# Third mixer of a four-layer block: moving the last channel tile, the value projection and the convolution's layer norm between the attention heads

## The chip, the cores and the metric

One core of a Trainium2 chip runs the whole program in one launch. The metric is the device time of one execution in microseconds (us). The engines are TensorE (PE, matrix products and transposes; PEld is its weight load), VectorE (DVE), ScalarE (ACT), GpSimd (POOL) and SyncE (SP, which here only issues transfers). PE writes into PSUM, which the kernel divides into eight banks of 128 x 512 floats.

## What is computed

A residual stream of 512 positions by 1024 channels passes four layers. The third layer's mixer, the one that the change touches, computes differential attention in 4 heads beside a convolution over 512 channels. Cut to what matters:

```python
def even_mixer_2(t, ...):
    proj = t @ w_in                                   # q, k, v, and a, g for the convolution
    y_a = diff_attention(proj[..., :3 * DIFF_WIDTH], ...)
    y_b = conformer_conv(proj[..., 3 * DIFF_WIDTH:], dw_w, dw_b, ln_g, ln_b)
    return jnp.concatenate([y_a, y_b], axis=-1) @ w_out

def diff_attention(...):     # 4 heads, two score maps each
    sc = jnp.einsum('bqhcd,bkhcd->bhcqk', qb, k) * scale
    p = jax.nn.softmax(jnp.where(chunk_causal_mask(i, s), sc, -jnp.inf), axis=-1)
    w = p[:, :, 0] - lam * p[:, :, 1]
    o = jnp.einsum('bhqk,bkhe->bqhe', w, v)
    ...
    o = rmsnorm(o, subln) * (1.0 - lam_init)

def conformer_conv(g, dw_w, dw_b, ln_g, ln_b):
    u = g[..., :CONV_CHANNELS] * jax.nn.sigmoid(g[..., CONV_CHANNELS:])
    y = lax.conv_general_dilated(u, dw_w, ...) + dw_b  # 31 taps, each channel by itself
    return jax.nn.silu(layernorm(y, ln_g, ln_b))
```

## The kernel before

Every projection is made in three passes over rounded parts of its operands (`mm3`, L143 to L149: high times high, high times low, low times high), so 512 columns against 1024 rows of input cost 8 x 3 matmuls. `projT` (L155) gives channels on the partitions, `projS` (L168) positions on the partitions. `wload` (L122) loads a piece of weights over SP into `wr`, ACT casts it to the high part (L133) and DVE subtracts to get the low part (L116).

The Python text is not the order in which the engines work. A framework places every instruction on its engine's queue: it goes by rank, which is the place in the program's text (moved ahead by `prio(n)`, behind by a negative one), and takes the first in rank that is ready on its own clock. Each queue then runs in the order so fixed, and semaphores guard the data. `hold` (L269) adds an edge of order without a semaphore. So work that stands later in the text fills the gaps of work that stands earlier. Buffers come from rings: 14 large tiles (`A4`), 13 of 512 columns (`U`), and PSUM banks in four rings, P (2), Z (3), W (2) and O (1).

`even2` (L722 to L899) is the third mixer. Its parts:

- `projT("e2t", ...)` with `conv` (L768) makes the convolution's input in four channel tiles of 128; the sigmoid is L777, the product `up` L778. Tiles 0 to 2 are convolved on DVE, 31 taps each (`taps`, L787 to L790), at low rank. Tile 3 goes to PE: `shifted` (L743) writes `up` to DRAM (L747), reads it back as four shifted copies `cu` (L752), and `conv_pe` (L758) makes 32 matmuls into bank O, `pc` (L764), which DVE adds to `ycv` (L766).
- `scores(h)` (L815) makes head h's two score maps in four blocks of 128 positions: products into two Z banks (L822), maximum and exponential (`softmax_rows`, L416 to L420), scaling and difference (L827 to L831), transposes into a W bank (`pw`) and a copy into `wt` (`evac_wt`, L361).
- `projS("e2v", ...)` (L885) is the value projection, through the two P banks. `av_(h)` (L839) multiplies `wt` with `v` into bank P (even heads) or O (odd heads), `po` (L368); ACT squares it (L378) and copies it (L379), DVE sums (L380).
- `stats` (L842) transposes `ycv` through W banks (L847), ACT copies to `yS` and squares (L849, L851). `norm` (L858) is the layer norm's root and the scaling (L861). `silu` (L863) transposes back through W banks, applies SiLU (L870) and splits into the two parts `mh`, `ml`.
- `heads` (L873) divides by the heads' norm (`over_rms`, L391), transposes through W banks, scales and splits (L881, L882). Then `outp` multiplies the mix with the output weights; `y` needs all eight banks, and its first channel tiles are the convolution's (order 4, 5, 6, 7, 0, 1, 2, 3). Four of its weights are cast into large tiles, `wb`.

The order of the text at the end of `even2` is scores(0), value projection, scores(1), channel tile 3, scores(2), av_(0), av_(1), the convolution on PE, scores(3), av_(2), stats, av_(3), norm, silu, heads.

Of the kernel before, what the change touches and what calls it, by code (L numbers as in the profile page):

```python
# [50 lines left out]
class Net:  # L51
# [670 lines left out]
    def even2(self):  # L722
        nc = self.nc
# [31 lines left out]
            nc.sync.dma_start(dwd, self.A["dwd"])  # L755
            cp[t] = us, dwd.rearrange("p a (m g c) -> p (a m) g c", g=4, c=32)

        def conv_pe(t):  # L758

            us, dwd = cp[t]  # L760
            pc = self.bank("O", "pc")
            for m in range(8):
                for g in range(4):
                    nc.tensor.matmul(pc[32 * g : 32 * g + 32], lhsT=dwd[:, m, g], rhs=us[g][:, 4 * m : 4 * m + 512],  # L764
                                     start=m == 0, stop=m == 7)
            V.tensor_scalar(ycv[:, t], pc, self.v("db", t), None, ALU.add)  # L766

        def conv(i, ps):  # L768
# [46 lines left out]
        def scores(h):  # L815
            wt = self.A4(name="wt")
            for tb in range(NB):
                N = (tb + 1) * P
                es = []
                rr = self.st(2, "rr")  # L820
                pss = [self.bank("Z", "sc") for _ in range(2)]
                self.pair([lambda r=slice(64 * c, 64 * c + 64), ps=ps: nc.tensor.matmul(  # L822
                    ps[:, :N], lhsT=qk[0][r, h, tb * P : N], rhs=qk[1][r, h, :N], start=True, stop=True) for c, ps in enumerate(pss)])
                for c, ps in enumerate(pss):
                    e, sm = self.softmax_rows(ps, N)
                    self.freed = self.freed or self.last_e
                    V.reciprocal(rr[:, c : c + 1], sm)  # L827
                    es.append(e)
                V.tensor_scalar(rr[:, 1:2], rr[:, 1:2], nlam, None, ALU.mult)
                nc.scalar.activation(es[0][:, :N], es[0][:, :N], AF.Copy, scale=rr[:, 0:1])  # L830
                V.scalar_tensor_tensor(es[0][:, :N], es[1][:, :N], rr[:, 1:2], es[0][:, :N], ALU.mult, ALU.add)  # L831
                self.evac_wt(wt, es[0], tb)
            wts.append(wt)
# [5 lines left out]
        def av_(h):  # L839
            self.head(h, wts[h], v, on, ss, "PO"[h % 2])  # L840

        def stats():  # L842

            for tb in range(NB):
                pt = self.bank("W", "pt")
                for k in range(4):
                    self.tr(pt[:, k * P : k * P + P], ycv[:, k, tb * P : tb * P + P])  # L847
                c = slice(tb, tb + 1)
                nc.scalar.activation(yS[:, tb], pt, AF.Copy, accum_out=sm[:, c])  # L849
                V.tensor_scalar(nm[:, c], sm[:, c], -1.0 / 512, None, ALU.mult)  # L850
                nc.scalar.activation(self.junk(512), yS[:, tb], AF.Square, bias=nm[:, c], accum_out=sq[:, c])  # L851
# [3 lines left out]
        def mix_half(i):  # L855
            self.mh[i], self.ml[i] = self.A4(F32R, "mh"), self.A4(F32R, "ml")

        def norm():  # L858
            r = self.rstd_v(sq, 4, 512, LN_EPS)
            for tb in range(NB):  # L860
                V.tensor_scalar(yS[:, tb], yS[:, tb], nm[:, tb : tb + 1], r[:, tb : tb + 1], ALU.add, ALU.mult)  # L861

        def silu():  # L863
            mix_half(1)
            for k in range(4):
                pt = self.bank("W", "pt")
                for tb in range(NB):
                    self.tr(pt[:, tb * P : tb * P + P], yS[:, tb, k * P : k * P + P])
                m = self.U(name="m")
                nc.scalar.activation(m, pt, AF.Silu, bias=self.v("lnb", k), scale=self.v("lng", k))  # L870
                self.split(*self.mix(4 + k), m)

        def heads():  # L873
            mix_half(0)
            self.over_rms(on, ss)
            for h in range(4):
                pt = self.bank("W", "pt")
                for tb in range(NB):
                    self.tr(pt[:, tb * P : tb * P + P], on[:, tb, h * P : h * P + P])
                mh, ml = self.mix(h)  # L880
                nc.scalar.activation(mh, pt, AF.Copy, scale=sub)  # L881
                V.scalar_tensor_tensor(ml, pt, sub, mh.bitcast(F32), ALU.mult, ALU.subtract)  # L882

        scores(0)
        self.projS("e2v", 512, lambda tb, ps: nc.scalar.copy(v[:, tb], ps))  # L885
        scores(1)
        self.projT("e2t", range(6, 8), conv)
        scores(2)
        av_(0)
        av_(1)  # L890
        conv_pe(3)
        scores(3)
        av_(2)
        stats()
        av_(3)
        norm()
        silu()
        heads()
        self.order = [4, 5, 6, 7, 0, 1, 2, 3]  # L899

# [546 lines left out]
```

## Time and profile before

| what | us |
|---|---|
| median of 3 runs (1713.58 to 1717.89) | 1717.76 |
| the profiled execution | 1711.21 |
| its span | 1709.4 |
| PE busy | 1656.5 |
| DVE busy | 950.2 |
| ACT busy | 677.7 |
| mean granted clock of PE (1 is full) | 0.987 |

The span is the time between the profile's first and last instruction; the execution has 1.8 us around it. Matmuls are pipelined and their ends are modelled, so a busy PE is not one at its peak. The third mixer's heads lie between about 607 and 710 us of the span.

### The profile page before, as it was taken

The page shows a single profiled execution, that of the slowest core. Times are in us where ns is not written, and L with a number is a line of the kernel's source. Part 1 is how long each engine was busy: PE and PEld are TensorE (multiplying, and loading weights), DVE is VectorE, ACT ScalarE, POOL GpSimd, SP SyncE. Part 2 cuts the span into 40 slices and gives each one's busy share as a digit, 9 for nine tenths or more (in the row PEclk, how much of TensorE's full clock was granted, in tenths as well). Part 3 has the DMA queues.
Part 4 walks back from the last instruction along what each step waited for, and adds up shares of the span by engine and source line. Part 5 has one row for each costly group of instructions (what it writes and reads, how often), then busy time and mean ns, then how long its engine had stood idle before and what let it go on. Part 6 is the DMA issues. An engine that isn't in the chain of part 4 may idle for free.

```text
span 1709.4 us, 20684 instructions
## 1 busy us (share of the span) xinstructions
PE 1656.5 (97%) x8072; PEld 1323.6 (77%) x8072; DVE 950.2 (56%) x1801; ACT 677.7 (40%) x1192; POOL 2.0 (0%) x8
## 2 busy tenths in 40 slices
PE   8999999999999999799999999999889999999998
PEld 8657788987789775588888878886447988888886
DVE  7564456765667994663222288468695622224332
ACT  6453334214545254643222254334556522223231
POOL 0000000000000000000000000000000000000000
PEclk9999999999999998899999999999999999999999
DMA  5212252202153220252222246432005332222341
GB/s 203 85 38 74 91 181 105 75 25 99 62 205 116 74 87 33 84 187 99 99 99 97 91 151 200 165 123 81 31 31 197 111 100 99 99 95 90 99 160 50
DMA packets 53169, 179.07 MB, mean 105 GB/s; under 512 B 5696, under 2 KB 8256, under 8 KB 52944
## 3 DMA queue, kind: packets, MB, share of 16 engines
q1 hardware_dynamic: 43824, 146.20, 25.6%
q10 hardware_dynamic: 9216, 31.48, 4.9%
q8 instruction: 63, 1.03, 0.2%
q14 instruction: 34, 0.28, 0.1%
q0 software_dynamic: 32, 0.07, 0.0%
HBM read 159.63 MB, written 18.10 MB: 104 GB/s over the span
## 4 chain that ended last, share of the span: by engine, by line
PE 85%; DVE 7%; ACT 4%; DMA 2%; issue 1%; ACTq 0%; DVEq 0%; SPq 0%
PE pp L145 17%; PE pp L148 17%; PE pp L149 17%; PE y L145 7%; PE y L149 7%; PE y L148 7%; PE pt L203 2%; PE po L368 2%; PE pl L625 1%; PE pw L203 1%; PE sc L822 1%; PE po L481 1%; DMA wr<-in_e2out 1%; PE pc L764 0%; DMA nw<-in_nw 0%
## 5 line engine op out<-in xcount | busy, mean ns | idle before, releaser
L116 DVE TENSOR_TENSOR wl<-wr,wh 128x1024 fp32r<-128x1024 f32 (+2 forms) x224 | 271.3, 1213 | 343.8 <-ACT wh L133 338.5
L133 ACT CAST wh<-wr 128x1024 fp32r<-128x1024 f32 (+2 forms) x224 | 233.4, 1043 | 523.4 <-PE pp L148 399.2
L148 PE MATMUL pp<-xl,wh 128*128 128x512 f32 (+1 forms) x1184 | 428.5, 362 | 0.0
L145 PE MATMUL pp<-xh,wh 128*128 128x512 f32 (+1 forms) x1184 | 426.0, 361 | 1.2 <-ACT xh L235 1.2
L149 PE MATMUL pp<-xh,wl 128*128 128x512 f32 (+1 forms) x1184 | 425.8, 360 | 0.0
L145 PEld LDWEIGHTS pp<-xh,wh 128*128 128x128 f32 x1184 | 223.8, 190 | 35.6 <-ACT xh L235 2.5
L148 PEld LDWEIGHTS pp<-xl,wh 128*128 128x128 f32 x1184 | 224.7, 190 | 33.8 <-issue 1.9
L149 PEld LDWEIGHTS pp<-xh,wl 128*128 128x128 f32 x1184 | 224.4, 190 | 33.4 <-issue 2.1
L145 PE MATMUL pp<-wh,xh 128*128 128x512 f32 (+1 forms) x320 | 126.4, 395 | 1.4 <-ACT sg L777 1.4
L148 PE MATMUL pp<-wl,xh 128*128 128x512 f32 (+1 forms) x320 | 126.5, 395 | 0.0
L149 PE MATMUL pp<-wh,xl 128*128 128x512 f32 (+1 forms) x320 | 125.4, 392 | 0.0
L145 PE MATMUL y<-wh,ah 128*128 128x512 f32 x288 | 112.7, 391 | 0.2
L148 PE MATMUL y<-wl,ah 128*128 128x512 f32 x288 | 112.3, 390 | 0.0
L149 PE MATMUL y<-wh,al 128*128 128x512 f32 x288 | 112.2, 389 | 0.0
L1238 DVE TENSOR_TENSOR act<-g,pp 128x512 f32<-128x512 f32 x44 | 30.2, 686 | 132.8 <-PE pp L149 131.4
L145 PEld LDWEIGHTS pp<-wh,xh 128*128 128x128 f32 x320 | 60.2, 188 | 13.4 <-ACT sg L777 1.8
L148 PEld LDWEIGHTS pp<-wl,xh 128*128 128x128 f32 x320 | 60.3, 188 | 11.7 <-issue 1.1
L149 PEld LDWEIGHTS pp<-wh,xl 128*128 128x128 f32 x320 | 60.2, 188 | 11.5 <-issue 0.6
L145 PEld LDWEIGHTS y<-wh,ah 128*128 128x128 f32 x288 | 54.1, 188 | 12.4 <-ACT bbz L998 1.1
L322 DVE TENSOR_TENSOR yn<-y,nw 128x512 f32<-128x512 f32 x48 | 31.8, 686 | 56.9 <-ACT yn L320 52.7
L790 DVE SCALAR_TENSOR_TENSOR ycv<-up,vec,ycv 128x512 f32<-128x512 f32 x90 | 63.2, 739 | 0.4
L149 PEld LDWEIGHTS y<-wh,al 128*128 128x128 f32 x288 | 54.1, 188 | 11.1
(381 smaller groups left out, 2335.0 us busy)
## 6 DMA issues: line engine op xcount, KB each, us to landing
wr<-in_f0gu SPq DMA_DIRECT2D x44, 512.0 KB, 3.3
wr<-in_f1gu SPq DMA_DIRECT2D x44, 512.0 KB, 3.3
wr<-in_f0d SPq DMA_DIRECT2D x22, 512.0 KB, 3.6
wr<-in_f1d SPq DMA_DIRECT2D x22, 512.0 KB, 3.4
xd<-x ACTq DMA_DIRECT2D x20, 512.0 KB, 2.7
x<-xd ACTq DMA_DIRECT2D x20, 512.0 KB, 6.1
wr<-in_o1t SPq DMA_DIRECT2D x16, 512.0 KB, 3.6
nw<-in_nw ACTq DMA_DIRECT2D x12, 512.0 KB, 7.8
```

What stands on the lines that cost most here:

```text
L116: return self.nc.vector.tensor_tensor(l, src, h.bitcast(F32), ALU.subtract)
L133: c = nc.scalar.copy(h, raw)
L145: r = mm(out, lhsT=a[0], rhs=b[0], start=first, stop=False)
L148: mm(out, lhsT=a[0], rhs=b[1], start=False, stop=False)
L149: return mm(out, lhsT=a[1], rhs=b[0], start=False, stop=last)
L203: self.nc.tensor.transpose(out, in_, self.ident)
L322: nc.vector.tensor_tensor(yn[j], yb[b][j], postw[j], ALU.mult)
L368: self.nc.tensor.matmul(po[:, tb * P : tb * P + P], lhsT=wt[:, sb, tb * P : tb * P + P], rhs=v[:, sb, c], start=sb == 0, stop=sb == tb)
L481: nc.tensor.matmul(po[r, sb * P :], lhsT=sv[:, sb, h * 64 : h * 64 + 64], rhs=wt[:, sb, sb * P :], start=sb == 0, stop=sb == 3)
L625: nc.tensor.matmul(pl[:, c4 * 64 : c4 * 64 + 64].rearrange("p (n x) -> p n x", x=H), lhsT=k[:, c4 * P : c4 * P + P], rhs=rh, start=True, s ...
L790: V.scalar_tensor_tensor(y, up[:, j : j + 512], self.v("dw", 4 * j + t), y, ALU.mult, ALU.add)
L1238: nc.vector.tensor_tensor(act[k // 4][:, k % 4], g, ps, ALU.mult)
```

## The change

The calls at the end of `even2` are reordered: channel tile 3 comes behind scores(0), the convolution on PE and then the value projection behind scores(1), layer norm (`stats`, `norm`) behind scores(2), `silu` behind scores(3) and ahead of the value products 1 to 3. The convolution gets an edge of order: its first matmul of each of the four column groups is placed behind the last exponential of the head whose scores were written last in the text, head 1.

```diff
-        def conv_pe(t):
+        def conv_pe(t, after):
...
-                    nc.tensor.matmul(pc[32 * g : 32 * g + 32], lhsT=dwd[:, m, g], rhs=us[g][:, 4 * m : 4 * m + 512],
-                                     start=m == 0, stop=m == 7)
+                    r = nc.tensor.matmul(pc[32 * g : 32 * g + 32], lhsT=dwd[:, m, g], rhs=us[g][:, 4 * m : 4 * m + 512],
+                                         start=m == 0, stop=m == 7)
+                    if m == 0:
+                        self.hold(r, after)
...
         scores(0)
+        self.projT("e2t", range(6, 8), conv)
+        scores(1)
+        conv_pe(3, self.last_e)
         self.projS("e2v", 512, lambda tb, ps: nc.scalar.copy(v[:, tb], ps))
-        scores(1)
-        self.projT("e2t", range(6, 8), conv)
         scores(2)
+        stats()
+        norm()
         av_(0)
+        scores(3)
+        silu()
         av_(1)
-        conv_pe(3)
-        scores(3)
         av_(2)
-        stats()
         av_(3)
-        norm()
-        silu()
         heads()
```

## Rows read from the trace of the kernel before

**Rows 1.** The page, engines: busy us, share of the span, instructions.
```profile
PE 1656.5 (97%) x8072; PEld 1323.6 (77%) x8072; DVE 950.2 (56%) x1801; ACT 677.7 (40%) x1192; POOL 2.0 (0%) x8
```
**Rows 2.** Stretches: start:end, length, busy by engine (instructions), PE clock, DMA share, GB/s.
```profile
607.70:652.50 44.80, 44.70 (x203) 31.86 (x202) 37.14 (x100) 25.70 (x59) 0.00 (x0) 1.00 0.24 77
652.50:673.20 20.70, 17.46 (x87) 11.29 (x90) 10.07 (x38) 11.30 (x29) 0.00 (x0) 0.74 0.18 67
673.20:681.60 8.40, 8.40 (x66) 2.11 (x65) 1.08 (x5) 1.69 (x6) 0.00 (x0) 0.83 0.01 2
681.60:692.60 11.00, 8.64 (x48) 5.29 (x45) 8.06 (x26) 7.42 (x20) 0.00 (x0) 1.00 0.00 1
692.60:710.10 17.50, 10.32 (x51) 8.36 (x50) 10.65 (x39) 12.92 (x28) 0.00 (x0) 0.71 0.00 0
710.10:757.50 47.40, 46.59 (x217) 37.56 (x217) 29.07 (x42) 25.38 (x43) 0.00 (x0) 1.00 0.53 189
```
**Rows 3.** PE in order of time: start, us, line, tile out<-in, count [idle before].
```profile
652.47 0.49 PE L822 MATMUL sc<-kT,qT 64*128 64x128 f32 x4
652.89 4.73 PE L368 MATMUL po<-v,wt 128*128 128x128 f32 x40
...
673.13 8.48 PE L764 MATMUL pc<-cu,dwd 128*32 128x512 f32 x64
...
681.80 0.70 PE L822 MATMUL sc<-kT,qT 64*128 64x256 f32 x4
...
692.40 0.60 PE L203 MATMUL pt<-cst,ycv 128*128 128x128 f32 x4
...
702.07 1.96 PE L203 MATMUL pt<-cst,yS 128*128 128x128 f32 x8 [6.29 <-DVE yS L861]
```
**Rows 4.** Stretches, the clock: as in rows 2.
```profile
662.00:673.00 11.00, 9.28 (x27) 4.90 (x26) 5.58 (x19) 6.05 (x14) 0.00 (x0) 0.52 0.19 70
...
678.00:680.00 2.00, 2.00 (x24) 0.60 (x20) 0.00 (x0) 0.00 (x0) 0.00 (x0) 1.00 0.04 8
```
**Rows 5.** ACT in order of time, 624 to 712 us: columns as in rows 3.
```profile
624.66 0.59 ACT L885 COPY v<-pp 128x512 f32<-128x512 f32 x1 [1.45 <-PE pp L149]
...
653.19 1.28 ACT L420 ACT_TABLE_LOAD   x1
654.49 0.37 ACT L420 ACTIVATE e<-sc,nm 128x128 f32<-128x128 f32 x1
...
692.60 0.59 ACT L361 COPY wt<-pw 128x512 f32<-128x512 f32 x1 [1.08 <-PE pw L203]
...
698.48 0.59 ACT L378 ACTIVATE sq<-po 128x512 f32<-128x512 f32 x1
...
703.86 1.45 ACT L870 ACTIVATE m<-pt,vec 128x512 f32<-128x512 f32 x2 [3.01 <-PE pt L203]
705.20 1.13 ACT L119 CAST mh<-m 128x512 fp32r<-128x512 f32 x2
...
710.11 1.46 ACT L881 ACTIVATE mh<-pt,lqt 128x512 fp32r<-128x512 f32 x2 [1.40 <-PE pt L203]
711.46 2.93 ACT L133 CAST wb<-wr 128x1024 fp32r<-128x1024 f32 x3
```
**Rows 6.** DVE in order of time, first mixer, then third: columns as in rows 3.
```profile
222.71 0.17 DVE L194 TENSOR_SCALAR h<-hs 128x16 f32<-128x16 f32 x1
...
225.09 2.50 DVE L391 TENSOR_TENSOR oret<-oret,r 128x512 f32<-128x512 f32 x4
...
643.48 0.68 DVE L790 SCALAR_TENSOR_TENSOR ycv<-up,vec,ycv 128x512 f32<-128x512 f32 x1
...
653.39 0.68 DVE L778 TENSOR_TENSOR up<-sg,pp 128x512 f32<-128x512 f32 x1
```
**Rows 7.** SP's issue of `cu`, and GB/s in 40 slices of 654 to 672 us.
```profile
656.23 2.54 SPq L752 DMA_DIRECT2D cu<-cvd  x4
GB/s 0 0 338 281 0 0 0 0 0 0 101 96 82 96 101 96 96 101 96 96 101 101 96 96 101 106 101 101 101 106 96 96 101 96 86 14 0 0 0 0
```

## Prediction, made before the changed kernel was run

> **What bounds the kernel now.** The first page says that TensorE (PE) is busy for 97% of the span [rows 1]; a matmul-bound kernel can only gain where PE stands still or runs at its lower clock. So the second view is the table by stretches of the third mixer's end [rows 2], read for PE busy against length, and for the clock. From 607.7 to 652.5 us PE is full (44.70 of 44.80 us): heads 0 and 1 lie over the value projection and the last channel tile. From 710.1 us, in the output projection, it is full again (46.59 of 47.40). Between them lie 57.6 us with all the slack: head 2 (20.7 us, mean clock 0.74), the convolution as a block (8.4), the rest of head 3 (11.0) and the tail (17.5, PE busy 10.32, clock 0.71). I then read the orders of PE, ScalarE (ACT) and VectorE (DVE) in these stretches [rows 3, 5, 6].
>
> Four things stand out. One: the convolution block runs from 673.13 for 8.48 us, and head 3's next scores come only at 681.80 [rows 3]; meanwhile ACT is busy 1.69 us and DVE 1.08 of 8.4 [rows 2]. Two: the `ycv` transposes of the layer norm start at 692.40, after head 3's last scores, and the `yS` transposes at 702.07 after a 6.29 us wait [rows 3]. Three: ACT serves the last value product (`sq<-po`) only at 698.48, after the norm's passes [rows 5]. Four: the first head transpose is read at 710.11 and the weights `wb` are cast right behind it, at 711.46 [rows 5]. I take 710.11 as the milestone: what follows it hangs on it, through `wb` and through the W banks that the head transposes leave to `y`.
>
> **The change, part by part.** Nothing is removed or added except one ordering edge; three things move. PE's work is the same, so the sum is one of waits.
>
> (1) *Channel tile under head 0, value projection under head 1.* Each is filler of PE behind scores of higher rank; PE was full and stays so, with one exception. The projection's two P banks are held until `up` is written: 652.47 to 653.39 + 0.68 = 654.07 us in the trace [rows 3, 6], 1.6 us, covered there because PE had `po` in the O bank. After the change the value projection needs those P banks, and ACT must also switch its table for the sigmoid. Bounds 0 (head 1's scores fill it) and 2.9 (1.6 plus a table load of 1.28 [rows 5]); I take 1.5. The cover of DVE's taps (last row at 643.48 [rows 6]) is not lost: the taps still lie under heads 0 and 1, and the layer norm, which needs them, comes only behind head 2. On SP and in ACT's casts the tile's two pieces of weights swap places with the projection's four, the same number of each: nothing, as both are prefetched under the key projection.
>
> (2) *Convolution after head 1's last exponential.* It goes in front of the remaining value projection, on a PE that is at full clock: 64 instructions at the 24 per 2 us of 678 to 680 [rows 4] are 5.3 us; in place they took 8.48 [rows 3], at a mean clock of 0.83 [rows 2]. Between these bounds I take 6.0, nearer to the warm row. Its four `cu` loads need time: issued from 656.23, they move data until slice 35 of 40 of the DMA row, 670.2, which is 16 us after `up` [rows 7]. The channel tile takes the place of the first half of the value projection, which ended at 624.66 [rows 5]; a table load, the sigmoid and `up` on top make 627.5, so the loads land near 643.5. Head 1 can start at 625 too and, at 2.0 + 11.0 us for a head at full clock (part 3), has its last exponential near 638.5. On SP the block's six transfers also move past the prefetch of output weights, which can hold them while it waits for a buffer. PE is in order, so if the block is queued behind that exponential, the value projection behind it waits: bounds 0 and 5; I take 1.5, since there is other work that can be put in front. Head 2 then starts at 652.5 + 1.5 + 6.0 + 1.5 = 661.5 (before 652.47).
>
> (3) *Heads 2 and 3.* They took 652.5 to 692.6, 40.1 us [rows 2]. Off: the block, 8.4. Back on: head 3's first softmax that ran beneath the block, for which ACT was busy 1.69 us there [rows 2]: 2.0. Off: a part of the 4.73 us of `po` that stood in front of head 2's second score block [rows 3], since `v` is now fresh and the product no longer gets there first: bounds 0 and 3, I take 2. The clock: it was 0.52 from 662 to 673 [rows 4], after thin PE work, and came back only inside the block; head 3 then ran at 1.00 [rows 2]. Without the block nothing dense stands between the heads, so head 3 probably runs at the lower clock. Head 2 from 657.6 to 673.2 needed 15.6 us at it, head 3 from 681.6 to 692.6 needed 11.0 at full clock: bounds 0 and 4.6, I take 2.5. The layer norm's first half (16 transposes; ACT 4 copies and 4 squares, 5.3 us, from the copy's end at 692.60 + 0.59 to 698.48 [rows 5]) now stands in ACT's queue between heads 2 and 3, with head 3's exponentials behind it. ACT is idle for 9.4 of head 2's 20.7 us [rows 2], so bounds 0 and 5.3; I take 2. Sum: 40.1 - 8.4 + 2.0 - 2.0 + 2.5 + 2.0 = 36.2, so head 3's last copy comes at 697.7 (before 692.60, [rows 5]).
>
> (4) *The tail, from that copy to the first head transpose read, 17.5 us before.* The norm's 5.3 us of ACT and its DVE chain leave it. What is late next is `silu`, which the change ranks ahead of the value products 1 to 3. ACT: copy 0.5, table load 1.28, four `m` and four `mh` (1.45 + 1.13 for two [rows 5], 5.2) = 7.0; then square and copy of product 2 and the square of product 3 (0.59 each [rows 5], 1.6 with their overlap); the sum on DVE, one pass of 0.68; the 16-wide root alone 2.4 (222.71 to 225.09 in the first mixer) and the four products 2.5 [rows 6]; four transposes 0.60 [rows 3]. Together 14.8. Lower bound 8.6, if ACT takes the last product before `silu`: copy 0.6, half a product 1.2 (4.73 us were two, [rows 3]), square 0.6, then the same 6.2. Upper 19 (second rival). The milestone: 697.7 + 14.8 = 712.5, +2.4 us.
>
> (5) *Output projection.* `silu`'s tiles come first in its order and are ready well before the milestone, but that is no gain: `y` of the last row block needs the W banks and `wb` comes behind the heads, so PE can do the first tile's matmuls alone, which it does now too, and then pauses. The block before shows what a restart costs: a mean clock of 0.83 over 8.4 us [rows 2] is 1.4 us lost. Bounds 0 and 1.4; I take 0.6.
>
> In all +3.0 us. The profiled execution took 1711.2 (span 1709.4 and 1.8 around it), so 1714.2; the median of the runs, 1717.8, lies 6.6 above it, and I carry the difference over: **1720.8**.
>
> **A rule against the change.** Rows first: the switch from sigmoid to exponential at 653.19 costs one load of 1.28 us, and the exponential starts at its end, at 654.49 [rows 5]. The Trainium skill ("ScalarE: Activation LUTs", Rules for kernel authors) says to do all functions of one table set before switching, and under "What ACT_TABLE_LOAD costs" it gives about 2.66 us for a switch, a drain of 1.38 included. By that figure the silu's one switch in the tail would be 1.4 longer and the forecast 1722.2. No drain shows in these rows, so I keep 1.28.
>
> **The rivals.**
> *Gaps take it all (faster).* ACT idles 9.4 us in head 2 and 3.6 in head 3 [rows 2]; norm and silu together need 5.3 + 5.2. If the order puts them there without touching a softmax, and the clock holds: head 2 from 652.5 + 1.5 + 5.3 = 659.3, heads 31.7 (part 3 without clock and norm), tail 8.6: milestone 699.6, -10.5 us: 1707. For it: the idle time is there. Against it: in the trace the `ycv` transposes had their input one DVE pass after the block's end at 681.6 and came at 692.40, just behind the last score transposes, though PE idled between [rows 2, 3]: the W banks seem to be handed out in program order, and they still will be, which pins `silu` behind head 3.
> *The O bank (slower).* Value products 1 and 3 share the single O bank. Before, product 1 was emptied a whole head earlier than `silu`. Now `silu` ranks ahead of product 1. If its first `m` gets to ACT before product 1's square, the bank stays full until silu's end (7.0), then 1.1, then product 3 on PE (2.4 by the 4.73 us for two, [rows 3]), then 1.1 + 0.7 + 2.4 + 2.5 + 0.6 = 17.8, at the lower clock some 19: +4 on the forecast, 1725. It decides as soon as a silu is ready before head 3's last score block leaves ACT idle.
> *Silu among exponentials (slower).* If silus are dispatched one by one within head 3, each costs two loads of the row's 1.28 us, 2.6 us of ACT, up to 10.3 in all; with two thirds of it on the softmax path +7: 1728. This is the case that the Trainium skill's rule on table sets speaks of. Against it: the W order just named.
> *The block waits for its loads (slower).* Part (2) with its full 5 us and no filler: 1.5 becomes 5: 1724.5.
> *It doesn't do what it says.* Priorities decide the order, and the edge may bind nothing: 1718.
>
> **How the numbers follow.** Chances: forecast 0.36, gaps 0.28, O bank 0.15, loads 0.10, silu among exponentials 0.07, no effect 0.04. 0.3%, about what a measurement of this kernel can tell from no change, is 5.2 us: 1712.6 to 1722.9. Faster: 0.24 of the gaps' 0.28. Slower: 0.09 of the forecast (its own range is 1714 to 1727), 0.11 of the O bank, 0.08, 0.07: 0.35. Within: 0.41. The range 1706 to 1732 reaches to the faster rival and to the silu case, and leaves out the ends where several bounds meet.
>
> **What would show it.** Right: PE full until about 661, `pc` at full clock around 640 to 650, the clock near 0.5 from about 670 to the end of head 3, `ycv` transposes between heads 2 and 3, `yS` transposes just behind head 3's last score transposes, the milestone at 712 to 713. The forecast is wrong if head 2 starts before the value projection ends (then its filler lies in the gaps), if `yS` is transposed inside head 3, or if the clock stays at 1.00 there.

## The result and the profile after

The changed kernel's median is 1725.39 us (1721.5 to 1727.22, 5 runs) against 1715.22 (1711.83 to 1717.89, 5 runs) of the kernel before on the same chip: ratio 1.0058, 95% interval [1.0037, 1.0078]. It is slower by 10.2 us, where +3.0 was forecast.

The profiled executions lie further apart (spans 1725.4 and 1709.4). Not all of that is the change. The last block of the key projection, where the changed stage begins, is evacuated 2.65 us later already, and 4.0 us more come between 1126 and 1315 us, in a stage with the same work. Profiles of the kernels below show such steps too, whatever their order: 0.2 to 4.5 us ahead of the stage. So the stage alone is compared here, from that evacuation (`r<-pp` on ACT, 607.83 before, 610.48 after) to the milestone, the first head transpose read (`mh<-pt` on ACT, 710.11 and 722.43): 102.3 before, 112.0 after, +9.7.

The page's engines, in the changed kernel (busy us, share, instructions; before: [rows 1]):

```profile
PE 1665.4 (97%) x8072; PEld 1328.5 (77%) x8072; DVE 950.5 (55%) x1801; ACT 677.1 (39%) x1192; POOL 2.0 (0%) x8
```

The work is the same, and PE's busy share too: the page alone doesn't show where 10 us went. The stretches of rows 2, in the changed kernel (start:end, length, busy by engine, clock, DMA share, GB/s):

```profile
607.70:652.50 44.80, 43.00 (x189) 28.55 (x188) 39.33 (x102) 27.36 (x61) 0.00 (x0) 0.96 0.33 114
652.50:673.20 20.70, 20.70 (x120) 12.06 (x116) 4.97 (x22) 5.06 (x15) 0.00 (x0) 1.00 0.00 1
673.20:681.60 8.40, 8.40 (x51) 5.95 (x50) 4.83 (x19) 4.88 (x13) 0.00 (x0) 1.00 0.00 0
681.60:692.60 11.00, 6.66 (x35) 4.36 (x34) 4.56 (x24) 7.52 (x23) 0.00 (x0) 0.80 0.01 1
692.60:710.10 17.50, 11.56 (x36) 7.39 (x36) 8.99 (x30) 11.79 (x26) 0.00 (x0) 0.50 0.00 1
710.10:757.50 47.40, 43.03 (x187) 34.06 (x187) 29.04 (x49) 23.09 (x39) 0.00 (x0) 0.87 0.49 176
```

PE is now full, at full clock, up to 681.6, where it had 17.46 of 20.7 us at 0.74 before [rows 2]. The gain there is lost again behind it: from 681.6 PE is busy for under two thirds, and from 692.6 to 710.1 it runs at half its clock.

PE of the changed kernel in order of time (start, us, line, tile, count, idle before):

```profile
626.89 0.39 PE L149 MATMUL pp<-xh,wl 128*128 128x512 f32 x1
627.21 0.49 PE L824 MATMUL sc<-kT,qT 64*128 64x128 f32 x4
628.63 0.63 PE L203 MATMUL pw<-cst,e 128*128 128x128 f32 x4 [0.93 <-DVE e L833]
630.10 0.75 PE L145 MATMUL pp<-wh,xh 128*128 128x512 f32 x1 [0.84 <-ACT sg L779]
630.64 0.63 PE L148 MATMUL pp<-wl,xh 128*128 128x512 f32 x1
...
633.62 0.39 PE L149 MATMUL pp<-wh,xl 128*128 128x512 f32 x1
...
650.99 2.76 PE L764 MATMUL pc<-cu,dwd 128*32 128x512 f32 x18
653.68 0.66 PE L203 MATMUL pw<-cst,e 128*128 128x128 f32 x4
654.27 5.35 PE L764 MATMUL pc<-cu,dwd 128*32 128x512 f32 x46
667.71 0.49 PE L824 MATMUL sc<-kT,qT 64*128 64x128 f32 x4
...
676.67 0.48 PE L824 MATMUL sc<-kT,qT 64*128 64x128 f32 x2
...
682.21 0.60 PE L203 MATMUL pt<-cst,ycv 128*128 128x128 f32 x4
...
690.30 2.66 PE L824 MATMUL sc<-kT,qT 64*128 64x256 f32 x4 [3.61 <-ACT e L420]
...
704.29 2.00 PE L203 MATMUL pt<-cst,yS 128*128 128x128 f32 x8
...
713.21 2.39 PE L368 MATMUL po<-v,wt 128*128 128x128 f32 x20
```

ACT of the changed kernel, same columns:

```profile
628.15 1.28 ACT L779 ACT_TABLE_LOAD   x1
629.45 0.60 ACT L779 ACTIVATE sg<-pp 128x512 f32<-128x512 f32 x1
...
682.90 0.60 ACT L851 ACTIVATE yS<-pt 128x512 f32<-128x512 f32 x1
...
688.13 0.72 ACT L853 ACTIVATE j<-yS,ln 128x512 bf16<-128x512 f32 x1 [0.22 <-DVE ln L852]
...
689.79 0.37 ACT L420 ACTIVATE e<-sc,nm 128x128 f32<-128x128 f32 x1 [0.84 <-DVE nm L418]
...
693.71 0.47 ACT L420 ACTIVATE e<-sc,nm 128x256 f32<-128x256 f32 x1 [2.44 <-DVE nm L418]
...
704.53 0.59 ACT L361 COPY wt<-pw 128x512 f32<-128x512 f32 x1 [2.50 <-PE pw L203]
705.14 1.28 ACT L872 ACT_TABLE_LOAD   x1
706.43 1.45 ACT L872 ACTIVATE m<-pt,vec 128x512 f32<-128x512 f32 x2
...
711.17 0.61 ACT L378 ACTIVATE sq<-po 128x512 f32<-128x512 f32 x1
...
715.64 0.60 ACT L378 ACTIVATE sq<-po 128x512 f32<-128x512 f32 x1 [2.40 <-PE po L368]
...
722.43 1.27 ACT L883 ACTIVATE mh<-pt,lqt 128x512 fp32r<-128x512 f32 x2 [5.72 <-PE pt L203]
```

DVE of the changed kernel, same columns (`nm` is the maximum that an exponential needs):

```profile
688.98 0.17 DVE L194 TENSOR_SCALAR h<-ln 128x4 f32<-128x4 f32 x1 [0.88 <-ACT j L853]
...
689.47 0.28 DVE L418 TENSOR_REDUCE nm<-sc 128x1 f32<-128x128 f32 x1
...
691.36 1.92 DVE L863 TENSOR_SCALAR yS<-yS,ln,r 128x512 f32<-128x512 f32 x4
...
693.27 0.40 DVE L418 TENSOR_REDUCE nm<-sc 128x1 f32<-128x256 f32 x1
```

Three places are to be read from these rows. **Head 2** starts at 667.71: behind the gate's table load and a bank wait at 627 to 630 (the sigmoid `sg`, behind the load, is what reads the bank that PE waits for), and behind the 8.1 us of the convolution block. **Head 3** has its first exponential only at 689.79, behind the layer norm's sums on ACT (682.90 to 688.85). Its maximum stands behind the norm on DVE too: the first scores were made from 676.67 on, but `nm` comes at 689.47, after the start of the norm's root, which waits for the last of ACT's sums; and the maximum at 693.27 stands behind the norm's scaling (691.36, 1.92), so that ACT waits 2.44 for it inside head 3. **The tail** from head 3's last copy (704.53) to the milestone takes 17.9: product 1's square is served only at 711.17, behind silu, and only then does PE get the bank for the 20 matmuls of product 3 (713.21).

### The profile page after: what moved, and what is told of

It is laid out like the page before. It is cut to its first block, busy times and chain, and to the rows that moved or that the text cites. A ratio compares the mean times of both kernels' runs of the same rounds, so it can differ in the third digit from the quotient of the medians.

```text
span 1725.4 us, 20689 instructions
## 1 busy us (share of the span) xinstructions
PE 1665.4 (97%) x8072; PEld 1328.5 (77%) x8072; DVE 950.5 (55%) x1801; ACT 677.1 (39%) x1192; POOL 2.0 (0%) x8
## 4 chain that ended last, share of the span: by engine, by line
PE 83%; DVE 8%; ACT 4%; DMA 3%; issue 1%; DVEq 0%; SPq 0%; ACTq 0%
PE pp L145 17%; PE pp L148 17%; PE pp L149 17%; PE y L145 7%; PE y L149 7%; PE y L148 7%; PE pt L203 2%; PE po L368 2%; PE pl L625 1%; PE pw L203 1%; PE sc L824 1%; DVE wl L116 1%; PE po L481 1%; DMA wr<-in_e2out 1%; DMA nw<-in_nw 0%
```

## The experiments

The theory made from this trace: three things cost, and each by its place. The block and the bank wait put head 2 later; the norm stands in front of head 3; silu stands in front of products 1 to 3 and holds the O bank shut. Rivals: the exchange of projections or the block alone made the loss; the low clock made it; silu's work sets the tail in any order.

Each kernel is read in the same stage, cut at head 2's first score (PE), head 3's last copy (ACT) and the milestone. The numbers are differences of such starts, in us; the ratio is to the kernel before, which ran beside each set: 1715.3 with e1 to e4, 1716.3 with e5 to e8, 1714.0 with e9 to e12.

| kernel | head 2 starts | heads 2, 3 | tail | stage | median | ratio [95%] |
|---|---|---|---|---|---|---|
| before | 44.6 | 40.1 | 17.5 | 102.3 | 1715.2 | 1 |
| changed | 57.2 | 36.8 | 17.9 | 112.0 | 1725.4 | 1.0058 [1.0037, 1.0078] |
| e1: silu behind products | 57.2 | 37.0 | 12.7 | 106.9 | 1720.0 | 1.0029 [1.0015, 1.0043] |
| e2: norm back | 57.3 | 26.3 | 26.3 | 110.0 | 1724.2 | 1.0052 [1.0039, 1.0065] |
| e3: exchange alone | 49.0 | 31.9 | 17.4 | 98.3 | 1708.6 | 0.9959 [0.9944, 0.9974] |
| e4: projection under late heads | 36.8 | 37.9 | 26.5 | 101.2 | 1712.7 | 0.9988 [0.9975, 1.0000] |
| e5: e3, block over head 3 | 49.0 | 25.9 | 20.6 | 95.5 | 1707.9 | 0.9956 [0.9938, 0.9974] |
| e6: exchange and block | 55.7 | 25.0 | 17.6 | 98.4 | 1711.6 | 0.9972 [0.9956, 0.9989] |
| e7: before, no gate loads | 44.7 | 37.6 | 17.3 | 99.6 | 1712.7 | 0.9984 [0.9965, 1.0002] |
| e8: e6, norm under head 3 | 57.3 | 26.4 | 15.3 | 99.0 | 1711.4 | 0.9977 [0.9960, 0.9994] |
| e9: changed, own banks | 55.7 | 37.2 | 15.2 | 108.1 | 1723.7 | 1.0054 [1.0035, 1.0073] |
| e10: e1 with filler | 57.3 | 50.1 | 13.7 | 121.1 | 1734.1 | 1.0117 [1.0092, 1.0143] |
| e11: block over both heads | 49.0 | 27.1 | 19.6 | 95.7 | 1710.0 | 0.9972 [0.9955, 0.9989] |
| e12: e11, gate in the O bank | 46.1 | 27.1 | 19.2 | 92.3 | 1705.2 | 0.9947 [0.9931, 0.9962] |

**Which part costs: e3, e6, e2, e1.**

e3, the kernel before with the exchange alone:

```diff
 scores(0)
+projT("e2t", 6..8, conv)
+scores(1)
 projS("e2v")
-scores(1)
-projT("e2t", 6..8, conv)
 scores(2)
 ...
```

> The kernel before with one part of the change: the last channel tile and the value projection trade places, the convolution and the layer norm stay where they were. Theory 'the exchange itself costs': the value projection waits for the bank of the channel tile that the sigmoid reads, and its first matmuls run at half clock, as at 627 to 634 in the changed kernel: 3 to 4 over the kernel before, 1718 to 1719. Rival 'the exchange is free' (the wait is made up where the loads of the convolution come earlier): within 1.5 of the kernel before.

It gained: 0.9959. Both expectations fell, for both looked only at what the exchange puts in front of head 2. That is there (head 2 starts 4.3 later), but heads 2 and 3 are 8.2 shorter. PE in e3:

```profile
658.07 0.49 PE L822 MATMUL sc<-kT,qT 64*128 64x128 f32 x4
658.49 0.94 PE L368 MATMUL po<-v,wt 128*128 128x128 f32 x6
659.35 0.96 PE L822 MATMUL sc<-kT,qT 64*128 64x256 f32 x4
...
671.91 7.07 PE L764 MATMUL pc<-cu,dwd 128*32 128x512 f32 x64
```

The stretch of head 2 in e3:

```profile
658.00:672.00 14.00, 14.00 (x87) 9.70 (x90) 8.95 (x37) 10.53 (x30) 0.00 (x0) 1.00 0.00 0
```

In the kernel before, head 2's second score block stood behind 40 matmuls of `po` (4.73) and its exponentials behind the gate's loads [rows 3, 5], and the clock then fell to 0.52 [rows 4]; head 2 took 20.8 from first score to last copy. In e3 the products lie between the score blocks, the clock stays at 1.00, and the head takes 13.9.

e6 adds the block in front of head 2, but keeps norm, products and silu in the order before:

```diff
 scores(1)
+conv_pe(3, self.last_e)
 projS("e2v")
 scores(2)
 ...
-conv_pe(3)
 scores(3)
```

> Exchange and convolution block as in the changed kernel (block in front of head 2), but layer norm, products and silu in the order of the kernel before. Theory 'the terms add': the exchange gives 4.8 within the mixer, the block in front costs 2 (head 2 starts 8.3 later, heads 2 and 3 are 6.1 shorter), and the cost of the changed kernel comes from the order behind: 1711 to 1714. Rival 'the block in front of head 2 is what turned a gain into a loss': 1718 to 1722.

1711.6: the terms add, and the block is not the cause. It puts head 2 6.7 later than e3 does and makes heads 2 and 3 6.9 shorter; with a tail 0.2 longer that is 0.1 in all. PE's first matmuls after the bank wait, in e6:

```profile
629.25 0.50 PE L145 MATMUL pp<-wh,xh 128*128 128x512 f32 x1 [0.83 <-ACT sg L779]
629.58 0.40 PE L148 MATMUL pp<-wl,xh 128*128 128x512 f32 x1
```

After the same wait as at 630.10 in the changed kernel the clock was full here (0.40 instead of 0.63 for a matmul). Head 2's start is 1.5 sooner than in e1, e2 and the changed kernel, which have the same order up to there, so at one and the same clock the block costs some 1.6.

ACT's first exponential of head 3, in e6:

```profile
678.81 0.42 ACT L420 ACTIVATE e<-sc,nm 128x128 f32<-128x128 f32 x1
```

Head 3's stretch in e6, between the copies, at full clock:

```profile
679.30:690.40 11.10, 8.68 (x45) 5.34 (x45) 8.48 (x31) 8.56 (x26) 0.00 (x0) 1.00 0.01 2
```

e2 is the changed kernel with the norm back behind head 3's scores:

```diff
 scores(2)
-stats()
-norm()
 av_(0)
 scores(3)
+stats()
+norm()
 silu()
```

> The changed kernel with the layer norm's sums and its scaling put back behind head 3's scores (ahead of silu); all else as changed. Theory 'the norm stands in head 3's way': head 3, 22.1 from head 2's last copy to its own, falls to 15 to 16 (head 2 without it takes 14.7), and the stretch behind it grows from 17.9 to 23 to 25, since the 6 of the sums on ScalarE now stand there: 1724 to 1726, no gain from the place of the norm alone. Rival 'the norm between the heads is hidden, head 3 is slow for its half clock': head 3 stays 20 to 22 and the stretch grows by 6: 1730 to 1733.

1724.2, as the first theory had it: what head 3 gains (36.8 to 26.3 for both heads) comes back in the tail (17.9 to 26.3), so the place of the norm is worth 2 as long as silu stands ahead of the products. The two parts lie further apart than expected, though: from head 2's last copy (682.90 in e2) to its own, head 3 takes 11.4, and the tail is 26.3.

e1 is the changed kernel with silu behind them:

```diff
 scores(3)
-silu()
 av_(1)
 av_(2)
 av_(3)
+silu()
 heads()
```

> The changed kernel with one call moved: silu goes behind the products of heads 1 to 3, so that product 1 takes the single O bank before silu's part of ScalarE's queue. Theory 'O bank' (in the changed kernel product 3 waits for the bank until 713, and the stretch from head 3's last copy at 704.5 to the first transpose of a head's product at 722.4 is 17.9): the stretch falls to 10 to 13, the time to 1718 to 1721, 5 to 8 under the changed kernel. Rival 'silu's own work on ScalarE sets the stretch, in whatever order it stands': the stretch stays 17 to 19, the time 1725 with 1 either way.

1720.0, and the tail falls from 17.9 to 12.65. ACT in e1:

```profile
704.72 0.59 ACT L361 COPY wt<-pw 128x512 f32<-128x512 f32 x1 [0.76 <-PE pw L203]
708.56 0.60 ACT L378 ACTIVATE sq<-po 128x512 f32<-128x512 f32 x1 [3.25 <-PE po L368]
...
717.37 1.27 ACT L883 ACTIVATE mh<-pt,lqt 128x512 fp32r<-128x512 f32 x2 [1.57 <-PE pt L203]
```

The last product's square is at 708.56 here, 3.8 behind the copy; in the changed kernel it was 11.1 behind (715.64).

By these four the +9.7 of the stage is: exchange -4.0 (e3 against before), block +0.1 (e6 against e3), norm between the heads with silu behind +8.5 (e1 against e6, which differ in product 1's place too, behind head 3's scores in e1; 1.5 of the 8.5 is the clock at 630), silu in front +5.1 (the changed kernel against e1). The medians, each taken against the kernel before beside it, give -6.7, +2.0, +9.4 and +5.4.

**The bank or the rank: e9.**

```diff
-self.head(h, wts[h], v, on, ss, "PO"[h % 2])
+self.head(h, wts[h], v, on, ss, "PPOP"[h])
```

> The changed kernel, order untouched, with products 0, 1 and 3 in the two banks that the projections leave and product 2 in the single O bank, so that no product waits for another's bank while silu runs. It splits the 5 us that silu behind the products gained. Theory 'the bank': product 3's matmuls no longer start at 713 but behind head 3, its square follows product 2's at 712.6 and not at 715.6, the stretch behind head 3 falls from 17.9 to 13 to 15: 1720 to 1723. Rival 'the rank alone': the squares and copies of products 1 to 3 stand behind silu's 4.9 on ScalarE whatever bank they have, the stretch stays 17 to 18: 1725 with 1 either way.

The tail is 15.2, so half of what e1 took away (5.25) was the bank, 2.7, and the rest goes, by subtraction, with the rank. ACT in e9:

```profile
711.77 0.61 ACT L378 ACTIVATE sq<-po 128x512 f32<-128x512 f32 x1
...
713.68 0.65 ACT L378 ACTIVATE sq<-po 128x512 f32<-128x512 f32 x1
...
720.37 1.27 ACT L883 ACTIVATE mh<-pt,lqt 128x512 fp32r<-128x512 f32 x2 [5.57 <-PE pt L203]
```

The third square now follows at once, but all three still stand behind silu. The clock doesn't explain the difference: it was 1.00 behind the last copy in e9 and 0.50 in the changed kernel (704.53 to 712), but silu's first `m` starts 1.9 behind that copy in both. In the medians, each against the kernel before beside it, the gain is 0.5 (+9.7 after +10.2), which their intervals can't tell from none.

**The norm: e8, e10.** e8 is e6 with the norm's transposes in the projections' banks and behind head 3's scores in rank:

```diff
 scores(3)
+stats()            # its pt from bank "P" instead of "W"
 av_(2)
-stats()
+norm()
 av_(3)
-norm()
 silu()
```

> Exchange and convolution block as changed; the layer norm's transposes use the two banks that the projections have left, and stand behind head 3's scores in rank, so that the sums run in head 3's gaps instead of in front of the head or behind it; products 2 and 3, then silu, behind. Theory 'the norm is worth moving only where it can run beside the head': head 3 takes 12 to 16, the stretch behind it 10 to 14: 1703 to 1708. Rival 'ScalarE has no room in head 3, the 6 of the sums delay it one for one': head 3 takes 17 to 19 and the time is that of the same kernel with the norm behind, 1711 to 1714.

Between the two: head 3 takes 12.5, as the theory has it, but the stretch behind it 15.3 and the time 1711.4, which is the rival's. Heads and tail together are 41.7 against 42.7 of e6; the stage is 0.7 longer, with head 2 starting 1.6 later. The sums in head 3's gaps lengthen the heads by 1.4 and shorten the tail by 2.3: 0.9 in all, since the last transposes still wait for head 3's end and the norm's scaling behind them stays in the tail.

e10 should have told how much of head 3's length is the clock:

```diff
+def fill(after):       # 14 matmuls of ones into a bank of their own, held behind `after`
 ...
 activation(j, yS, Square)
+fill(j)
 ...
 evac_wt(wt, es[0], tb)
+if h == 3: fill(self.last_e)
```

> The changed kernel with silu behind the products (the kernel of 1720.0), with 112 matmuls of no use added between the parts of the norm's sums and behind head 3's blocks, to keep TensorE busy where its granted clock was 0.5 (692 to 710). It asks how much of the 11.2 by which the norm lengthens head 3 (22.3 against 11.1 without it) is the clock. Theory 'half': with the clock near 1 in head 3 the head takes 17 to 19: 1715 to 1718. Rival 'the queue on ScalarE alone': head 3 takes 21 to 23, 1719 to 1721; if the added matmuls stand in the way of head 3's own, more.

It doesn't tell. The added matmuls stood together in PE's queue, in front of the norm's last transposes:

```profile
683.75 10.01 PE L823 MATMUL fill<-ones 128*128 128x128 f32 x84
```

Head 3 took 36.3, and these rows are the most of it. The split isn't settled by an experiment. What the traces say is against the clock: in the second half of head 3 it was 0.83 in e9 (697.30 to 705.14) and 0.50 in the changed kernel (697.00 to 704.53), and that half took 7.8 in e9, where matmuls of product 3 lie in it too, and 7.5 in the changed kernel.

**Why the exchange gains: e7, e12.**

```diff
-nc.scalar.activation(sg, ps, AF.Sigmoid)
+nc.scalar.activation(sg, ps, AF.Copy if t == 3 else AF.Sigmoid)
```

> The kernel before with one function changed: the gate of the last channel tile is a copy instead of a sigmoid, so that neither of the two table loads (650.43 and 653.19, 1.28 each) stands in ScalarE's queue at head 2's start; that leaves the sigmoid of one channel tile out. It asks why the exchange gains. Theory 'the gate's loads at the start of head 2 cost, and the exchange takes them out': head 2, 20.8 from its first score to its last copy, takes 16 to 19, and the time falls by 2 to 5, to 1710 to 1713. Rival 'the 40 matmuls of products 0 and 1 that stand whole between head 2's first two blocks (4.73) cost, loads or not': head 2 stays 20 to 21, 1714 to 1716.

Heads 2 and 3 are 2.5 shorter (head 2: 20.8 to 18.3), though the products still stand whole between the first two blocks:

```profile
653.09 4.73 PE L368 MATMUL po<-v,wt 128*128 128x128 f32 x40
```

So without the gate's loads head 2 loses 2.5 of the 6.8 by which e3 shortens it. That this is the loads' own time isn't shown: the first exponential follows the head's first score by 1.7 instead of 2.0, the second copy into `wt` by 11.2 instead of 11.6, and the rest comes behind that, in queues whose order is another without the loads. The remaining 4.3 go with the products' order and the clock (0.53 from 662 to 673 in e7), which no run here separates. The ratio's interval reaches just past 1.

e12 moves the gate's half of the channel tile to the O bank, in e11 (below):

```diff
-self.projT("e2t", range(6, 8), conv)
+self.projT("e2t", range(6, 8), conv, tags="PO")
```

> The same kernel as the one with the block over both heads, with the gate half of the last channel tile in the O bank, so that the value projection's first block finds a projection bank free. It measures the wait of the exchange by itself (TensorE idle 627.3 to 630.5 where the bank was awaited, and up to 10 matmuls at half clock behind). Theory 'the wait is on the path': head 2 starts 2 to 3.5 earlier, measured from the key projection's end (49.0 before), and the time is 2 to 3.5 under the kernel beside it. Rival 'the wait is made up where head 1's chain on VectorE is waited for': the same time within 1.

Head 2 starts 2.9 earlier, as the theory has it, and the stage is 3.4 shorter; the median is 4.8 under e11's, more than expected. PE in e12:

```profile
625.87 0.39 PE L149 MATMUL pp<-xh,wl 128*128 128x512 f32 x1
...
626.61 0.50 PE L145 MATMUL pp<-wh,xh 128*128 128x512 f32 x1
```

The value projection's first matmul starts 0.35 behind the tile's last one's end (626.26), where it waited 2.8 in the changed kernel (627.28 to 630.10). The bank wait was on the path.

**Dense work for the late heads: e4, e5, e11.** e4 leaves the value projection to heads 1 and 2 and the block to head 3:

```diff
 scores(1)
-conv_pe(3, self.last_e)
-projS("e2v")
 scores(2)
-stats(); norm(); av_(0)
+h2 = self.last_e
+projS("e2v")
 scores(3)
-silu(); av_(1); av_(2); av_(3)
+conv_pe(3, h2)
+av_(0); av_(1); av_(2); stats(); av_(3); norm(); silu()
```

> The changed kernel's channel tile under head 0, but the value projection is left to fill heads 1 and 2 and the convolution's block to fill head 3; products, layer norm and silu behind it in the order of the kernel before. Theory 'dense work has to be left for the late heads' (in the changed kernel heads 2 and 3 stand alone, 36.8 from head 2's first score to head 3's last copy, TensorE busy under half of head 3 and at half clock): head 3's last copy at 671 to 678 instead of 704.5, then 18 to 27 for products, norm and silu: 5 to 13 under the kernel before, 1702 to 1710. Rival 'ScalarE and VectorE set the heads and the dense work only stretches them': each head takes 19 or more under dense work, and the time stays within 3 of the kernel before, 1712 to 1718.

The rival's time came out, 1712.7. Head 2 takes 19.8 under the projection (13.9 with only products beside it), and all the products are left for the end: the tail is 26.5.

e5 is e3 with the block ranked behind head 3's scores:

```diff
+h2 = self.last_e     # behind scores(2)
 av_(0); av_(1)
-conv_pe(3)
 scores(3)
+conv_pe(3, h2)
```

> The exchange of projections alone (the kernel that gained 6.7), with the convolution's 64 matmuls ranked behind head 3's scores and not ahead of head 2's last exponential, so that they fill head 3's gaps instead of standing in front of its second block. Theory 'the block costs what stands uncovered': head 3, which took 18.0 between copies with the block in front (672.0 to 690.0), takes 13.5 to 14.5, as with the block spread in the kernel that left dense work for the late heads; the stretch behind it stays 17 to 18: 4 to 5 under the exchange alone, 1703 to 1705. Rival 'the spread block only pushes product 2 and product 3 behind the head': the stretch grows by as much as the head shrinks: 1708 to 1710.

The head shrinks more than the first theory says; its stretch in e5:

```profile
673.80:685.80 12.00, 12.00 (x76) 3.81 (x80) 7.75 (x30) 7.70 (x23) 0.00 (x0) 1.00 0.01 2
```

12.0 us, PE full, at full clock (e3: 18.0 between the same copies). But the tail grows by 3.2, since the block and product 2 end later; 2.8 of 6.0 stay. The median, 1707.9, lies at the rival's lower edge and can't be told from e3's.

e11 lets the block start behind head 1 and takes it ahead of product 1:

```diff
-h2 = self.last_e; av_(0); av_(1); scores(3); conv_pe(3, h2)
+h1 = self.last_e      # behind scores(1)
+av_(0); scores(3); conv_pe(3, h1); av_(1)
```

> The kernel with the block spread over head 3 (1707.9), with the block free from head 1's last exponential on and ahead of product 1 in the O bank, so that it fills gaps of heads 2 and 3 and is done when head 3 ends. Theory 'the stretch behind head 3 (20.6 there, 17.4 to 17.6 where the block was done) waits for the block's end': heads 2 and 3 stay at 26, the stretch falls to 17 to 18.5: 2 to 3 less, 1704 to 1706. Rival 'what is left behind the head is products instead of block, as long': 1707 to 1709.

The rival held in the stage: products instead of block lie behind the head, heads +1.1, tail -1.0, the stage as e5's. The median, 1710.0, is above both ranges. e12, on its basis, is the fastest of all: 0.9947 [0.9931, 0.9962], faster than both kernels of the case.

## Why the prediction was wrong where it was

The measured 1725.4 lies inside the range (1706 to 1732), against 1720.8 as the likeliest, but the +10.2 is over three times the +3.0 that was summed, and it came by the mechanism of a rival in the tail and by terms that make up for one another in the heads. Term by term, the stage against its forecast:

**(1) The bank wait, 1.5 (bounds 0 to 2.9): measured 2.9** (e12 against e11), the upper bound: between the channel tile's end (627.28) and 630.10 PE had head 1's first scores (0.49) and one transpose group (0.63) to fill it, then nothing else was ready. Half of the cost is no wait at all but the restart: eight matmuls from 630.10 on at half clock. The term had no such part, so that the bound fits is chance. Left out was the other side of the exchange, that the gate's loads and the products' block leave head 2. The prediction had the rows of both and booked only 2.0, for the products.

**(2) The block, 6.0: measured 8.1** (2.76 + 5.35 at clock 1.00). This step failed by a misread row. The 24 instructions per 2 us of rows 4 are all those that touch the window: 676 to 678 has 20 and 678 to 680 has 24, but 676 to 680 has 40. 64 in 7.07 (e3) is the rate at full clock, 0.11 each. **The loads, 1.5: measured 0.** They were issued at 635.42. GB/s in 40 slices of 634 to 652 us of the changed kernel:

```profile
GB/s 10 19 0 0 0 0 38 0 48 101 101 86 101 96 96 96 106 106 96 106 96 106 96 96 101 101 96 96 106 101 101 106 77 5 0 0 0 0 0 0
```

The traffic ends in slice 34, by 649.3, before the block starts at 650.99, close to head 1's last exponential, where the edge of order had placed it. In all head 2 started 12.6 later, not 9.0. The two terms are 11.0 of it; in the remaining 1.6 nothing waits (e12, without wait and with the block behind, still starts head 2 1.4 later than the kernel before, with PE busy for 46.08 of 46.23 us), and what it is stays open.

**(3) Heads 2 and 3, 36.2: measured 36.8, by luck a right sum of wrong terms.** Without norm and low clock the prediction had 31.7; e6 has 25.0. That is the exchange again, head 2 at 13.9 instead of 20.8. The norm was put at 2.0 with 5.3 as its upper bound, since ACT idles for 9.4 in head 2. This step failed. Up to head 3's first exponential alone the norm cost 8.6: from head 2's first score to head 3's first exponential it is 22.1 (667.71 to 689.79), and 13.5 in e6 (665.35 to 678.81). ACT's idle time in head 2 was of no use, for the sums' transposes came only behind head 2's last ones (682.21), and then head 3's softmax had to queue behind all eight passes, on ACT and, by its maximum at 689.47, on DVE. The rest of head 3, 14.7 against 11.6 in e6, is 3.2 longer, at clock 0.50 instead of 1.00, and the forecast had 2.5 for the clock. But the rows have another cause for the most of it: the wait of 2.44 at 693.71, for the maximum that stands behind the norm's scaling on DVE. The prediction counted the norm on ACT and left its DVE passes in the heads at nothing. What the clock cost in head 3 isn't shown.

**(4) The tail, 14.8: measured 17.9.** The rival "the O bank" had 17.8 to 19, and it is what happened: silu at 706.43 ahead of product 1's square at 711.17, then product 3 on PE at 713.21, its square at 715.64. The failed step was the count of ACT's queue alone, without the bank: with banks of their own for the products the tail is 15.2 (e9), near the 14.8. That the rival's 1725 is the measured time is in part chance, since head 2's start missed by 3.6 as well.

**(5) The restart, 0.6: measured none.** At the second evacuation of the last `y` block in the output projection (759.32 before) the profile is 9.4 later, the 2.65 taken off, 0.3 less than at the milestone, though the clock was 0.87 in that stretch.

The other rivals: "gaps take it all" failed, as the reason given against it had said: `yS` was scaled by 693.28, but transposed only at 704.29, just behind head 3's last score transposes, though PE had waited in between. But its picture, dense work that keeps head 2 at 13.9 and full clock, is what the exchange alone brings. "Silu among exponentials" did not come; there is one switch, 705.14 + 1.28, and `m` starts at 706.43. By the Trainium skill ("ScalarE: Activation LUTs", What ACT_TABLE_LOAD costs) it would have been 2.66 with a drain of 1.38; the copy before it ends at 705.12, so this trace shows no drain here either, and the measurement decides.

Of the signs, the `ycv` and `yS` transposes came where forecast and PE was nearly full until 681.6. Wrong were `pc` at 640 to 650 (651 to 660), the clock near 0.5 from 670 (1.00 until 681.6, 0.50 from 692.6) and the milestone (722.4, or 719.8 without the 2.65).

## What to carry to other kernels

A stage that moves into the gaps of a softmax must fit the gaps by its own releases, not by their sum: ask when its first input is ready and what then queues behind it, on every engine that it uses. Before ranking work ahead of a product, look which bank the product holds and who waits for that bank. A change of several moves is best run move by move: here one move gained 7 us, one was nearly even, two cost 15 together, and their sum told nothing of any.

## What the runs showed of the hardware

In front of the same matmuls, and behind the same idle time, the granted clock was at one or the other of its levels: 0.51 from 630.10 to 633.60 in the changed kernel (0.63 us a matmul), 1.00 from 629.25 to 632.80 in e6 (0.40 us) and from 631.90 to 635.40 in e9, each time behind 0.93 and some 0.84 us of waiting with little work. It moved head 2's start by 1.5 us between kernels with the same order up to there, so a difference of that size between two profiles needs a look at the clock first.
